# Seven block products instead of eight in a quarter of the down projection's K, in a one-core hybrid encoder layer

## The chip, the cores and the metric

The kernel runs on one core of one Trainium2 chip, in one launch. The metric is the device time of an execution in microseconds. The engines have short names in the profile: PE is TensorE (matmuls), PEld its weight loads, DVE is VectorE, ACT is ScalarE, POOL is GpSimd, SP is the engine that issues most DMAs.

## The reference, cut to what matters

One encoder layer over 256 tokens of width 2048, in float32. Three gated branches (a state-space mixer, dilated attention, a convolution module) are merged and projected; then comes the MLP, which is where the change is.

```python
h = rms_norm(x, norm1_g)
proj = h @ w_in                       # 2048 -> all branch inputs and gates
...                                   # three branches, gated and summed: merged
x = x + merged @ w_out
x = x + jnp.square(jax.nn.relu(rms_norm(x, norm2_g) @ w_mlp_up)) @ w_mlp_down
```

`w_mlp_up` is 2048 x 8192, `w_mlp_down` 8192 x 2048. Inputs and output are float32.

## The kernel before, in words

Weights are streamed from HBM in *units*: 256 rows of K by 512 columns, laid out as a tile of 128 partitions x 1024 (`raw`, 512 KB; two K chunks of 128 rows side by side). Each unit is split in two tiles of the matmul's own 32-bit type: ScalarE copies `raw` to `hi` (L1233) and VectorE subtracts, `lo = raw - hi` (`split_lo`, L254). Activations are kept as such pairs too. A product of two float32 values is then three matmuls: hi x hi, lo x hi and hi x lo (L1295, L1296, L1298 where the tokens are stationary and the weights stream, L1286, L1288, L1290 where the weights are stationary). A unit is 12 matmuls of 128x128 by 512 columns in the first mode (2 K chunks x 2 halves `t` of the tokens x 3); `ps` 0 runs the eight that need `hi`, then `ps` 1 the four that need `lo`.

Eight units make a *block*: a K of 2048 and 512 output columns for all 256 tokens, in two PSUM banks (`main`). The MLP's 8192 hidden values are cut in four parts r of 2048. An up block `("U", r, i)` gives 512 hidden values, and `job_up` turns them into squared ReLU activations `u` and their parts `ah`, `al` (one slab each, 4 K chunks x 256 tokens). A down block `("D", r, i)` multiplies part r's activations with 512 columns of the down weights, and `job_down` adds the result to `oacc[i]`, which began as x after the first half (`x` in the profile), and in the last part stores it. The order is U0 U1 D0 U2 D1 U3 D2 D3, each four blocks. A stretch of four down blocks is called a down stretch here.

The order of all instructions is written out by one loop over the units, with `k` the current unit (`for k in range(NU)`, L1326 on): load unit k+5 on SP's queue (`load`, L1215, 5 `raw` buffers), split unit k+3 (`LEAD` is 3; 4 `hi` and 4 `lo` buffers), run unit k's matmuls (`mm`), then let a planner (`Sched`) issue steps of the pending jobs behind them. So the `hi` of unit k+3 takes the buffer of unit k-1. Each engine runs its instructions in this order; semaphores hold what is not ready.

The planner's jobs are generators that yield their next need: `"v", n` or `"a", n` asks n ns of VectorE or ScalarE credit, `"w", n` waits n units, `"m", n` asks for n of 33 slabs of 4 KB a partition, `"b", n` for n of 4 PSUM banks, `"j", f` waits until f is true. A step of the highest priority (0: all MLP jobs) goes out while the credit is above 0, which it may then overdraw. Each unit ends with

```python
S.tick({"v": (2600 - 1140) * f * VSHARE, "a": (2600 - 950) * f * ASHARE, "g": 2600 * f, "p": 900})
...
self.credit[k] = min(self.credit[k] + g, CAP * max(g, 400.0))
```

with both shares 0.95 and `CAP` 1.2: a full unit brings VectorE a credit of 1387, and no more than 1664 are saved. `S.require` makes the planner issue whatever it takes, credit or not, until a condition holds (a slab, a bank or an accumulator that a job still has to give back).

PSUM has eight banks: two `main` tiles of two banks, used in turn (block b waits until block b-2 has been read), and four single banks (`pd`) for other work; the last block of all takes two of these.

Of the kernel before, what the change touches and what calls it, by code (L numbers as in the profile page):

```python
# [12 lines left out]
F32 = mybir.dt.float32  # L13
# [7 lines left out]
P = 128  # L21
# [169 lines left out]
def kernel(ctx: ExitStack, tc: tile.TileContext, xT, xn, par, cm, cd, cq, w1, wq, ws, out):  # L191
# [869 lines left out]
        st["rbc2"] = rb  # L1061


    act = {}

    def job_up(main, r, i):
        yield "m", 3
        u = slab([4, T], name="u")
        h = slab([4, T], F32R, name="ah")
        l = slab([4, T], F32R, name="al")  # L1070
        yield "j", lambda: "rbc2" in st
        yield "w", 1
        for e in range(2):
            yield "v", 680
            V.scalar_tensor_tensor(u[:, 2 * e:2 * e + 2, :], main[:, e, :].rearrange("p (a b) -> p a b", a=2), 0.0,
                                   st["rbc2"][:, None, :].to_broadcast([P, 2, T]), op0=ALU.max, op1=ALU.mult)
        st["main_free"].add(id(main))
        yield "w", 1
        yield "a", 1900
        A.activation(u, u, AF.Square)  # L1080
        A.activation(h, u, AF.Copy)
        yield "w", 1
        yield "v", 1150
        split_lo(l, u, h)
        S.give()
        act[r][0][i] = h
        act[r][1][i] = l

    def job_down(main, r, i):
        if r < 3:  # L1090
            yield "j", lambda: oacc[i] is not None
            yield "w", 1
            for t in range(2):
                yield "v", 620
                V.tensor_tensor(oacc[i][:, t, :], oacc[i][:, t, :], main[:, t, :], op=ALU.add)
            st["main_free"].add(id(main))
            return
        for t in range(2):
            V.tensor_tensor(oacc[i][:, t, :], oacc[i][:, t, :], main[:, t, :], op=ALU.add)  # L1099
            (nc.sync, nc.scalar)[t].dma_start(out[t * P:t * P + P, i * 512:i * 512 + 512], oacc[i][:, t, :])  # L1100
        st["main_free"].add(id(main))
        yield "w", 0


    st.update(h=([None] * 4, [None] * 4), ssd=([None] * 4, [None] * 4), conv=([None] * 4, [None] * 4),
              main_free=set(), conv_t=set(), q_blocks=0, att_n=0, ssd_c=[0] * 4, ssd_n=0, z_n=0, z_g=[False] * 4, mg_n=0,
              mgp=([None] * 4, [None] * 4), x2g=([None] * 4, [None] * 4))
    yss = cp.tile([P, 2, 4], F32, name="yss")
    st["yss"] = yss
# [67 lines left out]
    def up_block(r, i):  # L1177
        act.setdefault(r, ([None] * 4, [None] * 4))
        block("W", lambda: st["x2g"], lambda m: [(job_up(m, r, i), 0)],
              end=(lambda: S.give(8)) if (r == 3 and i == 3) else None)  # L1180

    def down_block(r, i):
        block("X", lambda: act[r], lambda m: [(job_down(m, r, i), 0)],
              end=(lambda: S.give(8)) if i == 3 else None)

    for o in ORDER:
        k, i = o[0], int(o[1])
# [7 lines left out]
        (up_block if k == "U" else down_block)(r, i)  # L1195


    units = [(bi, u) for bi, b in enumerate(blocks) for u in range(b["units"])]
    NU = len(units)
    raws, his, los = {}, {}, {}  # L1200

    def load(k):
        if k >= NU:
            return
        bi, u = units[k]
# [10 lines left out]
        raws[k] = t  # L1216

    def split(k):
        if k >= NU:
            return  # L1220
        bi, u = units[k]
        n = 2 * blocks[bi]["n"]
        h = hp.tile([P, 1024], F32R, tag="hi", name=nm("hi"))[:, :n]
        l = lp.tile([P, 1024], F32R, tag="lo", name=nm("lo"))[:, :n]
        r = raws.pop(k)
        if k == 0:
            for e in range(2):
                es = slice(e * n // 2, (e + 1) * n // 2)
                prep(e)
                A.activation(h[:, es], r[:, es], AF.Copy)  # L1230
                split_lo(l[:, es], r[:, es], h[:, es])
        else:
            A.activation(h, r, AF.Copy)  # L1233
            split_lo(l, r, h)
        his[k], los[k] = h, l
        S.on_split(k, n / 1024)

    mains = {}

    class Pair:  # L1240
# [5 lines left out]
        def __getitem__(self, at):  # L1246
            return self.of[at[1]][:, at[2]]

    def mm(k):
        bi, u = units[k]  # L1250
        b = blocks[bi]
        n, nk = b["n"], 2 * b["units"]
        if u == 0:
            if bi >= 2:
                j = mains[bi - 2]
                S.require(lambda: id(j) in st["main_free"], f"block {bi - 2} read")
                st["main_free"].discard(id(j))
            mains[bi] = pm.tile([P, 2, 512], F32, tag="main", name=nm("main")) if bi + 1 < len(blocks) \
                else Pair(bank(), bank())
        main = mains[bi]  # L1260
        wh = his.pop(k).rearrange("p (a b) -> p a b", a=2)
# [12 lines left out]
        first, last = kcs[0] == 0, kcs[1] == nk - 1  # L1274
        tail = bi == len(blocks) - 1 and u == b["units"] - 1
        order = [(ps, e, kc, t) for ps in range(2) for e, kc in enumerate(kcs) for t in range(2)]
        if tail:
            order.sort(key=lambda o: o[3])
        for ps, e, kc, t in order:
            ah, al = hi[kc // 4][:, kc % 4, :], lo[kc // 4][:, kc % 4, :]  # L1280
            if b["mode"] == "W":
                for c in (2 * t, 2 * t + 1):
                    o = main[:, t, (c % 2) * T:(c % 2) * T + T]
                    cs = slice(c * P, c * P + P)
                    if ps == 0:
                        PE.matmul(o, wh[:, e, cs], ah, start=(first and e == 0 and c % 2 == 0), stop=False,  # L1286
                                  skip_group_check=True)
                        PE.matmul(o, wh[:, e, cs], al, start=False, stop=False, skip_group_check=True)  # L1288
                    else:
                        PE.matmul(o, wl[:, e, cs], ah, start=False, stop=(last and e == 1), skip_group_check=True)  # L1290
            else:
                o = main[:, t, :n]
                xs_ = slice(t, T, 2) if b["perm"] else slice(t * P, t * P + P)
                if ps == 0:
                    PE.matmul(o, ah[:, xs_], wh[:, e, :], start=(first and e == 0), stop=False)  # L1295
                    PE.matmul(o, al[:, xs_], wh[:, e, :], start=False, stop=False)  # L1296
                else:
                    PE.matmul(o, ah[:, xs_], wl[:, e, :], start=False, stop=(last and e == 1))  # L1298
        if u == b["units"] - 1:
            if b["end"]:  # L1300
                b["end"]()
            for g, pr in b["post"](main):
                S.add(g, f"block{bi}", pr)

    S.take(8)
    st["xg"] = ([slab([4, T], F32R, name="xgh") for _ in range(4)], [slab([4, T], F32R, name="xgl") for _ in range(4)])
# [8 lines left out]

    for i in range(5):
        load_x(i)
        load(i)
    for i in range(LEAD):
        if i:  # L1320
            prep(2 * i)
# [2 lines left out]
    S.add(job_h(), "h", 0)  # L1324
    for k in range(NU):
        load_x(k + 5)  # L1326
        load(k + 5)
# [12 lines left out]
        bi, u = units[k]  # L1340
# [80 lines left out]
```

## Time and profile before

| | |
|---|---|
| three runs | 1958.81, 1959.17, 1960.99 us; median 1959.17 |
| the profiled execution | 1958.74 us, span of the trace 1957.0 us |
| granted TensorE clock | 0.999 |
| busy | PE 1945.3, PEld 1750.7, DVE 1302.9, ACT 1021.7, POOL 59.6 us |
| DMA | 373.03 MB, mean 191 GB/s |

Times in the profile count from the start of the span. A row of a group reads: line, engine, operation, output and inputs, shapes, count, then busy time in us and mean duration of one in ns, then the engine's idle time ahead of these instructions and what ended it. A row in time reads: start, duration, engine, line, operation; in brackets the idle time before it and what ended that. A row of a table by windows gives for each engine its busy time and its number of instructions in that stretch. Matmuls overlap in the array, so the duration of one is longer than the step from one start to the next.

### The profile page before, as it was taken

The page shows a single profiled execution, that of the slowest core. Times are in us where ns is not written, and L with a number is a line of the kernel's source. Part 1 is how long each engine was busy: PE and PEld are TensorE (multiplying, and loading weights), DVE is VectorE, ACT ScalarE, POOL GpSimd, SP SyncE. Part 2 cuts the span into 40 slices and gives each one's busy share as a digit, 9 for nine tenths or more (in the row PEclk, how much of TensorE's full clock was granted, in tenths as well). Part 3 has the DMA queues.
Part 4 walks back from the last instruction along what each step waited for, and adds up shares of the span by engine and source line. Part 5 has one row for each costly group of instructions (what it writes and reads, how often), then busy time and mean ns, then how long its engine had stood idle before and what let it go on. Part 6 is the DMA issues. An engine that isn't in the chain of part 4 may idle for free.

```text
span 1957.0 us, 29897 instructions
## 1 busy us (share of the span) xinstructions
PE 1945.3 (99%) x11738; PEld 1750.7 (89%) x11738; DVE 1302.9 (67%) x1878; ACT 1021.7 (52%) x1390; POOL 59.6 (3%) x74
## 2 busy tenths in 40 slices
PE   9999999999999999999999999999999999999999
PEld 9999999999989788888888888999988998998887
DVE  6688888787888888987655555555554554555444
ACT  7665586756666645544554444544443443444332
POOL 0000001000000000002000000000000000000000
PEclk9999999999999999999999999999999999999999
DMA  9575555565556555555565555555555555555554
GB/s 328 164 238 184 159 186 192 176 202 176 193 188 195 181 170 183 189 188 192 182 195 189 187 194 204 189 188 188 189 193 185 191 186 192 190 187 190 187 181 151
DMA packets 108174, 373.03 MB, mean 191 GB/s; under 512 B 12288, under 2 KB 13056, under 8 KB 108032
## 3 DMA queue, kind: packets, MB, share of 16 engines
q1 hardware_dynamic: 103904, 360.23, 55.8%
q0 software_dynamic: 2560, 8.39, 1.5%
q10 hardware_dynamic: 1568, 2.49, 0.4%
q8 instruction: 92, 1.51, 0.3%
q14 instruction: 50, 0.41, 0.1%
HBM read 368.84 MB, written 2.23 MB: 190 GB/s over the span
## 4 chain that ended last, share of the span: by engine, by line
PE 65%; DVE 0%; issue 0%
PE main L1295 15%; PE main L1296 15%; PE main L1298 15%; PE main L1286 6%; PE main L1290 6%; PE main L1288 6%; PE b L990 1%; PE b L1296 0%; PE b L1295 0%; PE b L1298 0%; DVE mg L973 0%; DVE x L1099 0%; PE b L608 0%; PE b L295 0%; PE b L635 0%
## 5 line engine op out<-in xcount | busy, mean ns | idle before, releaser
L254 DVE TENSOR_TENSOR lo<-raw,hi 128x1024 fp32r<-128x1024 f32 (+2 forms) x697 | 832.6, 1196 | 627.4 <-ACT hi L1233 622.1
L1233 ACT ACTIVATE hi<-raw 128x1024 fp32r<-128x1024 f32 (+2 forms) x695 | 715.2, 1031 | 855.6 <-PE main L1296 473.7
L1295 PE MATMUL main<-hi,hh 128*128 128x512 f32 (+1 forms) x800 | 303.4, 379 | 0.0
L1296 PE MATMUL main<-hi,hl 128*128 128x512 f32 (+1 forms) x800 | 297.3, 372 | 0.0
L1286 PE MATMUL main<-x2h,hi 128*128 128x256 f32 x1024 | 245.1, 280 | 0.0
L1288 PE MATMUL main<-x2l,hi 128*128 128x256 f32 x1024 | 244.3, 279 | 0.0
L1286 PE MATMUL main<-hh,hi 128*128 128x256 f32 x896 | 217.1, 282 | 2.8 <-ACT hi L1233 2.8
L1288 PE MATMUL main<-hl,hi 128*128 128x256 f32 x896 | 214.7, 280 | 0.0
L592 DVE SCALAR_TENSOR_TENSOR co<-cin,cpar,co 128x256 f32<-128x256 f32 x480 | 206.9, 483 | 0.0
L1298 PE MATMUL main<-lo,hh 128*128 128x512 f32 (+1 forms) x800 | 200.0, 372 | 0.0
L1288 PEld LDWEIGHTS main<-x2l,hi 128*128 128x128 f32 x1024 | 193.1, 189 | 0.2
L1286 PEld LDWEIGHTS main<-x2h,hi 128*128 128x128 f32 x1024 | 192.7, 188 | 0.2
L1295 PE MATMUL main<-hi,ah 128*128 128x512 f32 x480 | 188.9, 394 | 0.0
L1296 PE MATMUL main<-hi,al 128*128 128x512 f32 x480 | 188.6, 393 | 0.0
L1286 PEld LDWEIGHTS main<-hh,hi 128*128 128x128 f32 x896 | 169.1, 189 | 3.4 <-ACT hi L1233 3.2
L1295 PEld LDWEIGHTS main<-hi,hh 128*128 128x128 f32 x800 | 152.4, 190 | 21.7 <-issue 0.5
L1296 PEld LDWEIGHTS main<-hi,hl 128*128 128x128 f32 x800 | 152.5, 191 | 21.3 <-issue 0.9
L1288 PEld LDWEIGHTS main<-hl,hi 128*128 128x128 f32 x896 | 169.1, 189 | 0.2 <-issue 0.2
L1298 PEld LDWEIGHTS main<-lo,hh 128*128 128x128 f32 x800 | 147.8, 190 | 21.2
L1290 PE MATMUL main<-x2h,lo 128*128 128x256 f32 x1024 | 140.2, 280 | 0.0
L1298 PE MATMUL main<-lo,ah 128*128 128x512 f32 x480 | 130.1, 393 | 0.0
L1290 PEld LDWEIGHTS main<-x2h,lo 128*128 128x128 f32 x1024 | 128.5, 188 | 0.0
(242 smaller groups left out, 2255.9 us busy)
## 6 DMA issues: line engine op xcount, KB each, us to landing
raw<-ws_dram SPq DMA_DIRECT2D x600, 512.0 KB, 3.3
raw<-wq_dram SPq DMA_DIRECT2D x88, 384.0 KB, 3.2
fr<-sums POOLq DMA_DIRECT2D x32, 256.0 KB, 6.5
raw<-w_dram SPq DMA_DIRECT2D x7, 448.0 KB, 6.9
xr<-xn_dram SPq DMA_DIRECT2D x4, 512.0 KB, 7.9
x<-xn_dram SPq DMA_DIRECT2D x4, 512.0 KB, 4.3
xt<-xT_dram SPq DMA_DIRECT2D x7, 256.0 KB, 7.0
out_dram<-x SPq DMA_DIRECT2D x4, 256.0 KB, 3.6
```

Of the source, the lines that this page charges most:

```text
L254: V.tensor_tensor(lo, raw, hi.bitcast(F32), op=ALU.subtract)
L592: V.scalar_tensor_tensor(dst[:, e, :], x[:, e, k:k + T], par_("dw", (2 * i + e) * 31 + k), dst[:, e, :], op0=ALU.mult, op1=ALU.add)
L990: PE.transpose(b[:, e, t * P:t * P + P], src[:, t, k * P:k * P + P], ID)
L1233: A.activation(h, r, AF.Copy)
L1286: PE.matmul(o, wh[:, e, cs], ah, start=(first and e == 0 and c % 2 == 0), stop=False, skip_group_check=True)
L1288: PE.matmul(o, wh[:, e, cs], al, start=False, stop=False, skip_group_check=True)
L1290: PE.matmul(o, wl[:, e, cs], ah, start=False, stop=(last and e == 1), skip_group_check=True)
L1295: PE.matmul(o, ah[:, xs_], wh[:, e, :], start=(first and e == 0), stop=False)
L1296: PE.matmul(o, al[:, xs_], wh[:, e, :], start=False, stop=False)
L1298: PE.matmul(o, ah[:, xs_], wl[:, e, :], start=False, stop=(last and e == 1))
```

## The change

It rewrites only the down blocks, the accumulators and the planner's bookkeeping around them. The weights in HBM, their order in memory and every load's size stay.

Two neighbouring down blocks of a part (columns of i and i+1, i = 0 or 2) become one block of mode "Y", a *pair*. Of its eight K steps, steps 2 to 7 run as before, as *plain* units. In steps 0 and 1, that is, in a quarter of K, the four 512-column products of the two blocks are computed as a two-by-two block product (token halves x the two K chunks, times K chunks x the two column blocks) with seven block products in place of eight, in Winograd's form of Strassen's scheme. Each step becomes a *group* of four part-units that share the two raw tiles x (block i) and y (block i+1):

- part a: x is split as before; two products, one into the partial product p1, one straight into the first column block's accumulator. Behind the split, four sums of 128x512 are formed on VectorE: two in a slab `us`, one in place in y, one in place in x.
- part d: y, by now with its first half replaced by a sum, is split; two products.
- part b: `us` is split; two products.
- part c: the second half of x, by now a sum, is split (512 wide); one product.

So a group is 3 x (2 + 2 + 2 + 1) = 21 matmuls of 512 columns, where two units had 24. The stationary sides are the activations, or sums of their blocks, which `job_up` forms ahead for the first slab of each part (i = 0) in two slabs `sh`, `sl`, and which are kept until the part's last pair is done with them.

The units of a pair run in this order: four plain, a group, four plain, a group, four plain. The partial products p1, p5, p6, p7 take four more banks; with the two `main` tiles a pair thus has all eight. One pair has its accumulators in the `main` tiles and its partial products in the `pd` banks, the next the other way round; up blocks 2 and 3 of parts 1 to 3 take `pd` banks. `job_seven`, added after the second group's part c, reads the partial products: one copy on ScalarE and five additions or subtractions on VectorE, then three additions within SBUF, into `oacc`. `job_down` adds the accumulators as before; in the last part it waits until the pair's `job_seven` is done, and stores both token halves.

Loads follow the order of the raw tiles; x and y stay held until part c has been split. The planner's credit for VectorE is, per part-unit, `(2600 * e - 1140 * dv) * f * VSHARE` with (e, dv) = (0.5, 3.2) for a, (0.5, 1) for d and b, (0.25, 0.5) for c.

The core of the diff:

```diff
     def job_up(main, r, i):
...
+        if i == 0:
+            yield "m", 3
+            f = slab([4, 2, P], name="sf")
+            sh = slab([4, 2, P], F32R, name="sh")
+            sl = slab([4, 2, P], F32R, name="sl")
+            a = u.rearrange("p (q e) (t j) -> p t e q j", e=2, t=2)
+            for o, x, y_, op in ((0, a[:, 1, 0], a[:, 1, 1], ALU.subtract), (1, f[:, 0], a[:, 0, 0], ALU.subtract),
+                                 (2, a[:, 0, 0], a[:, 1, 0], ALU.subtract), (3, a[:, 0, 1], f[:, 1], ALU.add)):
+                yield "v", 400
+                V.tensor_tensor(f[:, o], x, y_, op=op)
+            yield "w", 1
+            yield "a", 950
+            A.activation(sh, f, AF.Copy)
+            yield "w", 1
+            yield "v", 1150
+            split_lo(sl, f, sh)
+            S.give()
+            acs[r] = sh, sl
...
+    def job_seven(p, done, i):
+
+        p1, p5, p6, p7 = p
+        yield "m", 1
+        tq = slab([2, 512], name="tq")
+        (c11, c21), (c12, c22) = [[oacc[i + e][:, t, :] for t in range(2)] for e in range(2)]
+        yield "w", 1
+        yield "a", 600
+        A.activation(tq[:, 0, :], p1, AF.Copy)
+        yield "v", 650
+        V.tensor_tensor(c11, c11, p1, op=ALU.add)
+        yield "v", 650
+        V.tensor_tensor(tq[:, 0, :], tq[:, 0, :], p6, op=ALU.add)
+        yield "v", 650
+        V.tensor_tensor(tq[:, 1, :], p5, tq[:, 0, :], op=ALU.subtract)
+        yield "v", 650
+        V.tensor_tensor(c21, c21, p7, op=ALU.add)
+        yield "v", 650
+        V.tensor_tensor(c22, c22, p7, op=ALU.subtract)
+        done()
+        for c, e in ((c21, 0), (c12, 1), (c22, 1)):
+            yield "v", 620
+            V.tensor_tensor(c, c, tq[:, e, :], op=ALU.add)
+        S.give()
+        st["seven"] += 1
...
+        for e, us in ((0, (2, 3)), (1, (2, 3)), (None, (0,)), (0, (4, 5)), (1, (4, 5)), (None, (1,)), (0, (6, 7)),
+                      (1, (6, 7))):
+            for u in us:
+                if e is None:
+                    order_ += [(bi, u), (bi, 8 + u)]
+                    for w in "adbc":
+                        units.append((bi, u, w, (len(order_) - 2, len(order_) - 1)))
+                else:
+                    order_.append((bi, 8 * e + u))
+                    units.append((bi, u + 8 * e, "n", (len(order_) - 1,)))
...
     def split(k):
...
+            if w in "na":
+                r = raws[rs[0]]
+            else:
+                r = {"d": raws[rs[1]], "b": sums[0], "c": raws[rs[0]][:, 512:]}[w]
             A.activation(h, r, AF.Copy)
             split_lo(l, r, h)
+        if w == "a":
+            S.require(lambda: S.mem >= 1, "slab for sums")
+            S.take()
+            sums[0] = slab([1024], name="us")
+            lo_, hi_ = slice(0, 512), slice(512, 1024)
+            x, y_, z = raws[rs[0]], raws[rs[1]], sums[0]
+            for o, p, q in ((z[:, lo_], x[:, lo_], y_[:, lo_]), (y_[:, lo_], y_[:, lo_], y_[:, hi_]),
+                            (z[:, hi_], z[:, lo_], y_[:, hi_]), (x[:, hi_], z[:, hi_], x[:, hi_])):
+                V.tensor_tensor(o, p, q, op=ALU.add)
...
+    def seven(k):
...
+        todo = {"a": ((A_(0, 0), f1, 0), (A_(1, 0), c1, 0)), "d": ((S_(3), f2, 1), (S_(4), c2, 0)),
+                "b": ((S_(1), f1, 1), (S_(2), f2, 0)), "c": ((A_(1, 1), c1, 1),)}[w]
+        for ps in range(2):
+            for i, ((xh, xl), o, t) in enumerate(todo):
+                cs = slice(512 * i, 512 * i + 512)
+                four = o is f1 or o is f2
+                if ps == 0:
+                    PE.matmul(o[:, t, :], xh, wh[:, cs], start=(four and u == 0), stop=False)
+                    PE.matmul(o[:, t, :], xl, wh[:, cs], start=False, stop=False)
+                else:
+                    PE.matmul(o[:, t, :], xh, wl[:, cs], start=False, stop=(four and u == 1))
...
-        S.tick({"v": (2600 - 1140) * f * VSHARE, "a": (2600 - 950) * f * ASHARE, "g": 2600 * f, "p": 900})
+        e, dv, da = {"n": (1, 1, 1), "a": (0.5, 3.2, 1), "b": (0.5, 1, 1), "d": (0.5, 1, 1), "c": (0.25, 0.5, 0.5)}[w]
+        S.tick({"v": (2600 * e - 1140 * dv) * f * VSHARE, "a": (2600 * e - 950 * da) * f * ASHARE, "g": 2600 * f * e,
+                "p": 900})
```

More of the change, by code (lines that the diff above doesn't have):

```diff
@@ L1061, in job_rms2, with free @@
         st["rbc2"] = rb
-    act = {}
+    act, acs = {}, {}
+    def free(main):
+        st["main_free"].add(id(main))
+        if isinstance(main, Pair):
+            S.banks += 2
     def job_up(main, r, i):
@@ L1076, in job_up @@
                                    st["rbc2"][:, None, :].to_broadcast([P, 2, T]), op0=ALU.max, op1=ALU.mult)
-        st["main_free"].add(id(main))
+        free(main)
         yield "w", 1
@@ L1097, in job_down @@
-            return
-        for t in range(2):
             V.tensor_tensor(oacc[i][:, t, :], oacc[i][:, t, :], main[:, t, :], op=ALU.add)
-            (nc.sync, nc.scalar)[t].dma_start(out[t * P:t * P + P, i * 512:i * 512 + 512], oacc[i][:, t, :])
-        st["main_free"].add(id(main))
-        yield "w", 0
+            if r == 3:
+                (nc.sync, nc.scalar)[t].dma_start(out[t * P:t * P + P, i * 512:i * 512 + 512], oacc[i][:, t, :])
+        free(main)
+    def job_seven(p, done, i):
[20 more added lines that the diff above has]
+            V.tensor_tensor(c, c, tq[:, e, :], op=ALU.add)
+        S.give()
+        st["seven"] += 1
@@ L1180, in up_block @@
               end=(lambda: S.give(8)) if (r == 3 and i == 3) else None)
+        blocks[-1]["apart"] = r > 0 and i >= 2
     def down_block(r, i):
-        block("X", lambda: act[r], lambda m: [(job_down(m, r, i), 0)],
-              end=(lambda: S.give(8)) if i == 3 else None)
+        if i % 2 == 0:
+            block("Y", lambda: act[r], None, units=16)
+            blocks[-1].update(r=r, i=i)
     for o in ORDER:
@@ L1247, in __getitem__, with pm_tile, pd_pair @@
             return self.of[at[1]][:, at[2]]
+    pms = []
+    def pm_tile():
+        if len(pms) >= 2:
+            j = pms[-2]
+            S.require(lambda: id(j) in st["main_free"], "accumulators read")
+            st["main_free"].discard(id(j))
+        pms.append(pm.tile([P, 2, 512], F32, tag="main", name=nm("main")))
+        return pms[-1]
+    def pd_pair():
+        S.require(lambda: S.banks >= 2, "banks read")
+        S.banks -= 2
+        return Pair(bank(), bank())
     def mm(k):
-        bi, u = units[k]
+        bi, u, w, _ = units[k]
         b = blocks[bi]
         n, nk = b["n"], 2 * b["units"]
[L1253 to L1259, printed above, removed]
+        pair = b["mode"] == "Y"
+        if bi not in mains:
+            if pair:
+                S.require(lambda: b["r"] in acs, "sums of activations")
+                make = pm_tile if b["i"] == 0 else pd_pair
+                mains[bi] = [make(), make()]
+            else:
+                mains[bi] = (pd_pair if b.get("apart") else pm_tile)()
+        if w != "n":
+            if (u, w) == (0, "a"):
+                make = pd_pair if b["i"] == 0 else pm_tile
+                b["four"] = [make(), make()]
+            seven(k)
+            return
         main = mains[bi]
+        if pair:
+            j, u = divmod(u, 8)
+            main = main[j]
+            nk = 16
         wh = his.pop(k).rearrange("p (a b) -> p a b", a=2)
@@ L1273, in mm @@
         hi, lo = parts(b["key"])
-        first, last = kcs[0] == 0, kcs[1] == nk - 1
-        tail = bi == len(blocks) - 1 and u == b["units"] - 1
+        first, last = kcs[0] == (4 if pair else 0), kcs[1] == nk - 1
+        tail = k == NU - 1
         order = [(ps, e, kc, t) for ps in range(2) for e, kc in enumerate(kcs) for t in range(2)]
@@ L1298, in mm @@
                     PE.matmul(o, ah[:, xs_], wl[:, e, :], start=False, stop=(last and e == 1))
-        if u == b["units"] - 1:
+        if pair:
+            if u == 7:
+                if j == 1 and b["i"] == 2:
+                    S.give(8)
+                S.add(job_down(main, b["r"], b["i"] + j), "down", 0)
+        elif u == b["units"] - 1:
             if b["end"]:
@@ L1317 @@
         load_x(i)
-        load(i)
+        load_upto(i)
     for i in range(LEAD):
@@ L1326 @@
         load_x(k + 5)
-        load(k + 5)
+        load_upto(k + 5)
         if k + LEAD < 8:
```

74 lines of the change are left out of this document (57 added, 17 removed).

## The prediction, made before the changed kernel was run

> **What bounds the kernel now.** I read the page's first two parts, then the chain of work that ended last, then a table by windows of the four down-projection stretches, then single instructions in time.
>
> ```profile
> PE 1945.3 (99%) x11738; PEld 1750.7 (89%) x11738; DVE 1302.9 (67%) x1878; ACT 1021.7 (52%) x1390; POOL 59.6 (3%) x74
> ...
> PE 65%; DVE 0%; issue 0%
> ```
>
> TensorE is busy in 1945.3 of 1957.0 us, and the chain is TensorE work with nothing to speak of from the others. But a busy share is an average, so the stretches that change are read alone.
>
> ```profile
> core 0: us, PE busy (x) PEld busy (x) DVE busy (x) ACT busy (x) POOL busy (x), PEclk, DMA share, GB/s
> 1419.10:1507.30 88.20, 88.20 (x383) 71.57 (x382) 45.13 (x41) 35.16 (x34) 0.00 (x0) 1.00 0.57 191
> 1600.50:1688.20 87.70, 87.70 (x390) 71.83 (x389) 44.31 (x40) 35.05 (x34) 0.00 (x0) 1.00 0.57 192
> 1777.50:1865.60 88.10, 88.10 (x383) 71.55 (x382) 44.36 (x41) 35.83 (x34) 0.00 (x0) 1.00 0.58 189
> 1865.60:1952.90 87.30, 87.23 (x381) 71.09 (x379) 40.42 (x39) 29.36 (x28) 0.00 (x0) 1.00 0.48 165
> ```
>
> In all four, TensorE has no idle time that counts and the full granted clock (1.00), weight loading leaves room, VectorE is half used (45.13 of 88.20 us), ScalarE 40%, the DMA engines 57%. So a matmul taken out there comes off the end, as long as the other engines stay ahead. What one matmul costs is not its duration (they overlap) but the step from one start to the next:
>
> ```profile
> 1419.13 0.40 PE L1295 MATMUL main<-hi,ah 128*128 128x512 f32 x1
> ...
> 1508.15 0.28 PE L1286 MATMUL main<-x2h,hi 128*128 128x256 f32 x1
> ```
>
> These are the first matmul of the first down stretch and the first of the up block behind it: 89.02 us for 4 blocks x 8 units x 12 = 384 matmuls, 231.8 ns each. Now one unit in detail:
>
> ```profile
> 1842.39 0.40 PE L1295 MATMUL main<-hi,ah 128*128 128x512 f32 x1
> ...
> 1844.01 0.39 PE L1296 MATMUL main<-hi,al 128*128 128x512 f32 x1
> ...
> 1844.23 1.08 PE L1298 MATMUL main<-lo,ah 128*128 128x512 f32 x4
> 1844.43 1.06 ACT L1233 ACTIVATE hi<-raw 128x1024 fp32r<-128x1024 f32 x1 [1.70 <-PE main L1296]
> ...
> 1845.15 0.39 PE L1295 MATMUL main<-hi,ah 128*128 128x512 f32 x1
> ...
> 1845.53 1.23 DVE L254 TENSOR_TENSOR lo<-raw,hi 128x1024 fp32r<-128x1024 f32 x1 [0.34 <-ACT hi L1233]
> ```
>
> A unit steps in 2.76 us (1842.39 to 1845.15), 230.0 ns a matmul; I use 231 ns, between the two. Three things more are to be seen. The last of the four L1298 starts at about 1844.92 and the next unit's first follows one step later: a unit boundary costs nothing. The ScalarE copy starts when the eighth matmul of the unit ends (1844.01 + 0.39 = 1844.40), as its hi buffer is then free, 0.92 us before the unit's steps end. And the lo, behind it on VectorE, ends 1.84 us after the unit's steps end (1845.53 + 1.23 - 1844.92), for a unit that TensorE reaches three units later. That lead of 6 us or more is the cover of all that follows.
>
> **The change, part by part.** *Matmuls removed.* In each of 4 down stretches, 2 chunk pairs, 2 K steps (units 0 and 1): two units of 12 become 3 x (2 + 2 + 2 + 1) = 21. So 16 groups x 3 = 48 matmuls less, all 128x512: 48 x 0.231 = 11.1 us, on the path. That is the gain and its upper bound; nothing else leaves TensorE.
>
> *Units cut smaller.* 64 part-units (a, d, b, c) in place of 32 whole ones: 32 boundaries more. By the row above they cost nothing. The dearest nearest row is a separate wait instruction in TensorE's queue:
>
> ```profile
> L1295 PEldq EVENT_SEMAPHORE  x3: 51/51/51, 684.7 to 694.8; - x3
> ```
>
> 32 x 51 ns = 1.6 us is the upper end; I take 0, as boundaries in these stretches show no such wait.
>
> *Work added to VectorE and ScalarE.* Prices, from the groups of VectorE and of ScalarE in the last two down stretches, and one group of the whole span for an addition of two 512-wide operands in SBUF:
>
> ```profile
> L254 DVE TENSOR_TENSOR lo<-raw,hi 128x1024 fp32r<-128x1024 f32 x61 | 74.5, 1225 | 79.3 <-ACT hi L1233 77.2 <-PE b L1296 2.1
> L1095 DVE TENSOR_TENSOR x<-x,main 128x512 f32<-128x512 f32 x8 | 5.1, 680 | 0.0
> L1099 DVE TENSOR_TENSOR x<-x,main 128x512 f32<-128x512 f32 x6 | 3.9, 683 | 3.9 <-PE main L1298 3.9
> L1075 DVE SCALAR_TENSOR_TENSOR u<-main,rbc 128x512 f32<-128x512 f32 x2 | 1.3, 680 | 0.0
> ```
>
> ```profile
> L1233 ACT ACTIVATE hi<-raw 128x1024 fp32r<-128x1024 f32 x60 | 63.3, 1059 | 100.7 <-PE main L1296 81.5 <-DMA raw<-ws_dram 9.0 <-DVE x L1099 8.7
> L1081 ACT ACTIVATE ah<-u 128x1024 fp32r<-128x1024 f32 x1 | 1.1, 1059 | 0.0
> L1080 ACT ACTIVATE u<-u 128x1024 f32<-128x1024 f32 x1 | 1.0, 1042 | 0.0
> ```
>
> ```profile
> L879 DVE TENSOR_TENSOR em<-em 128x512 f32<-128x512 f32 x16 | 11.0, 691 | 1.3 <-ACT em L872 0.3
> ```
>
> VectorE, per group: 3.5 lo in place of 2 (3 x 1.23 + 0.69 - 2 x 1.23 = 1.92) and 4 weight sums of 128x512 (4 x 0.69 = 2.76), so 4.7 us, x16 = 75. Per pair 8 additions at 0.68 = 5.4, x8 = 44. Per stretch, in the up stage before it, 4 sums of activations (256 wide, at most the 0.69 of 512) and a lo of 1.22, 4.0, x4 = 16. Together 135 us, all beside TensorE's work, if no single one is late. A pair takes 12 x 2.77 + 42 x 0.231 = 42.9 us, and two of them a stretch; VectorE's share there goes from 45 in 88 to about 45 + 19 + 11 = 75 in 86 us. ScalarE gets 1.5 hi per group and per pair a copy of half a hi's width, about 0.6, some 35 us in all with the four copies of the activation sums; never near its limit.
>
> *Is any of it late?* Zero is TensorE's start on part a; four plain units of 2.77 lie before it (ends at -8.31, -5.54, -2.77, 0), and a, d, b end at 1.39, 2.77, 4.16, c at 4.85. There are four hi and four lo buffers, so each part takes that of the unit four before it, at the times the unit above shows. hi(a) -9.23 to -8.17; lo(a) to -6.90; the sums to -4.14. hi(d) needs the second sum (-5.52), ends -4.46; lo(d) -2.91. hi(b) takes the third plain unit's buffer, -3.69 to -2.63; lo(b) -1.35. hi(c) -0.92 to -0.3; lo(c) 0.69. The next plain unit takes a's buffer: hi 0.92 (two thirds of a) to 1.98, lo to 3.25. Wanted: d at 1.39, b at 2.77, c at 4.16, the plain unit at 4.85. The smallest lead is 2.9 us, at the plain unit behind the group. In the first group after an up stage the last block's activations are in the way: two L1075 (0.68 each) ahead of lo(a); then, as the sums need a slab that only those activations give back, a square and a copy on ScalarE (1.04 and 1.06) and one lo ahead of the sums. The sums then end at -1.73, hi(d) at -2.05, lo(c) at 1.42, and the plain unit's hi still at 1.98: still 2.9 us. I cost it at nothing; without this cover each group would pay what it is late.
>
> *Accumulators.* Each pair takes eight banks, and the next block's first four are those that the pair's partial products held, read by six instructions that begin after the second c. The planner gives each VectorE job credit: a plain unit brings 1387 (at most 1664 saved), part a takes 2231, d and b bring 152, c 76. So 1664 before the group falls to -567, -415, -263, -187; the first plain unit brings 1200, and two additions of 650 go out; the second brings 1287, two more; the third 1374, the last one, and the banks count as free, before the fourth unit is issued. In time, from the end of c: the lo of the fourth plain unit ends 2.2, two additions 3.6, a lo 4.8, two additions 6.2, a lo 7.4, the last 8.1. The next block starts at 4 x 2.77 = 11.08: 3.0 us ahead of need. Nothing.
>
> *Loads.* Same bytes and the same 512 KB pieces, but both raw buffers of a group stay held until lo(c) has read the second column half (0.69). Behind that the SP queue loads the plain unit 4 after the group and the next group's first piece.
>
> ```profile
> raw<-ws_dram SPq DMA_DIRECT2D x600, 512.0 KB, 3.3
> ...
> out_dram<-x SPq DMA_DIRECT2D x4, 256.0 KB, 3.6
> ```
>
> 0.7 + 3.3 = 4.0, with two in flight perhaps 6; the fourth plain unit's hi can't start before part c's buffer is free, at 4.6, and TensorE reaches that unit at 4.85 + 3 x 2.77 = 13.2. Nothing. In the last stretch the first pair's output DMAs wait on SP and ScalarE behind both blocks' additions; the raws of the next group are queued ahead of them, and hi of the unit four ahead is put back to about 6.3 us after the end of the pair's last unit but one, 4.7 us before TensorE wants it. Nothing.
>
> *The end.*
>
> ```profile
> 1951.51 0.69 DVE L1099 TENSOR_TENSOR x<-x,b 128x512 f32<-128x512 f32 x1 [8.26 <-PE b L1298]
> ...
> 1952.22 0.34 SPq L1100 DMA_DIRECT2D out_dram<-x  x1
> 1952.87 0.69 DVE L1099 TENSOR_TENSOR x<-x,b 128x512 f32<-128x512 f32 x1 [0.67 <-PE b L1298]
> 1953.59 0.34 ACTq L1100 DMA_DIRECT2D out_dram<-x  x1
> ```
>
> The last halves are added and stored as before. But block 2's two stores now go out some 3 us before block 3's last instead of 20 us, since its last unit is two units before the end and three of the pair's additions precede it. With 3.6 us a landing they overlap the last store a little: 0 to 1.5 us, and I take 0.4, near the lower end, as only the last part of one store overlaps.
>
> *Sum.* The profiled execution took 1958.74 us (span 1957.0 and 1.74 around it): 1958.74 - 11.1 + 0.4 = 1948.0. The median of the runs shown, 1959.17, lies 0.43 higher: 1948.5.
>
> The Trainium skill's page "TensorE: Matmul & The Clock Gate", section "Back-to-back issue gap", speaks against this size: it gives about 131 ns a matmul for a sustained stream of weight loads and matmuls of 512 columns. By it 48 of them are worth 6.3 us and the time would be 1953.3. The trace disagrees with it, 231 ns in all 384 steps counted; I go by the trace.
>
> **The rivals.**
> *Part of the gain is lost in the groups* (small waits at part boundaries, about 0.1 us at each of 64, or VectorE late by 0.4 us in each of 16 groups): 6.4 us back, 1954.9 - against it, boundaries that cost nothing and 2.9 us of lead; for it, VectorE's share of nearly nine tenths around the groups and the longer chain copy, lo, sums, copy. With half as much, 1951.7.
> *The gain is cancelled or more by the accumulators: slower.* If the reads of the partial products go out only when the next block asks for their banks, they stand behind the lo that ends 1.84 us into that block, and five additions of 0.68 follow: TensorE waits 5.2 us at each of 7 pair ends (the eighth has no block behind it), 36.7 us, 1985. It decides from 11.1 / 7 = 1.6 us a pair on, which is 4.6 us later than my reckoning. The credit that falls to -567 speaks for it, the 1387 a plain unit against it. By the same page of the Trainium skill, section "Part 1: The HAM clock gate", idleness beyond some 3.4 us halves TensorE's clock, which would add to this; no row here shows such a gap.
> *A removed matmul brings less than the mean step.* If the step were held by something other than the streaming of its columns, what goes could be as little as its weight load, 71.57 us / 382 = 187 ns in the first window: 9.0 us, 1950.6, still inside the forecast's own range. What speaks against it is that weight loading has room in all four windows. The figure of the page named above would leave 1953.3, and no row supports it.
> *No change within the measurement*: a mix of late groups that returns 8 to 14 us, about 1959.
>
> **How the numbers follow.** A kernel measured here can be told from no change at about 0.2%, 3.9 us, so 1955.2 divides faster from same. The forecast (1947.0 to 1950.5) has 0.78; the partial loss 0.11, nearly all still faster; a step worth less than 187 ns 0.01; no change 0.05; slower 0.05. Faster 0.88, same 0.07, slower 0.05. The low end is the full 11.1 with no tail and the spread of the runs, the high end takes in the boundaries (1.6), the tail (1.5) and half the partial loss: 1946.8 to 1953.5.
>
> **What the profile of the changed kernel would show.** TensorE's matmuls 48 fewer, about 11690; each down stretch from its first matmul to the next stage 89.0 - 12 x 0.231 = 86.2 us; a group from a to the plain unit behind it 4.85 us against 5.54; TensorE's busy time equal to its window in all four; VectorE near 1438 us in all; the six reads of the partial products ending about 8 us after c. I am wrong if TensorE shows idle time before part d or before the plain unit behind a group (the sums are late), before the first matmul of a block (accumulators), or before hi at a raw (loads); or if the step of the part-units is not 231 ns.

## The result, and the profile after

| | before | changed |
|---|---|---|
| median | 1959.16 us (4 runs, 1958.81 to 1960.99) | 1949.19 us (4 runs, 1948.74 to 1949.48) |
| ratio, 95% interval | | 0.9947, 0.9930 to 0.9964 |
| profiled execution, span | 1958.74, 1957.0 us | 1948.74, 1947.0 us |

The change makes the kernel 10.0 us faster; 1948.5 was forecast. First the page of the changed kernel, parts 1 and 4:

```profile
PE 1935.5 (99%) x11690; PEld 1741.8 (89%) x11690; DVE 1419.1 (73%) x2058; ACT 1054.8 (54%) x1434; POOL 59.6 (3%) x74
...
PE 65%; DVE 0%; issue 0%
```

There are 48 matmuls fewer (11738 before), VectorE is 116 us busier, and the chain that ended last names TensorE for 65% of the span and nothing else to speak of, as before. The four down stretches in a table by windows (busy us and instructions of each engine, TensorE clock, DMA share, GB/s):

```profile
core 0: us, PE busy (x) PEld busy (x) DVE busy (x) ACT busy (x) POOL busy (x), PEclk, DMA share, GB/s
1419.10:1505.20 86.10, 86.10 (x374) 69.89 (x373) 70.73 (x80) 43.09 (x45) 0.00 (x0) 1.00 0.60 195
1594.90:1680.60 85.70, 85.70 (x373) 69.82 (x372) 70.66 (x80) 43.01 (x45) 0.00 (x0) 1.00 0.59 196
1770.20:1856.30 86.10, 86.10 (x374) 69.73 (x373) 70.51 (x80) 43.06 (x45) 0.00 (x0) 1.00 0.58 195
1856.30:1942.80 86.50, 86.50 (x374) 69.95 (x372) 68.53 (x80) 37.31 (x39) 0.00 (x0) 1.00 0.53 171
```

TensorE is busy for the whole of each window while VectorE's share went from a half to 82%: the added work is covered. How far the first stretch shrank is read from its first matmul and the first of the up block behind it, and the last two stretches from their first matmul (in the kernel before, then in the changed one) to the last addition:

```profile
1419.10 0.39 PE L1425 MATMUL main<-hi,ah 128*128 128x512 f32 x1
...
1505.30 0.28 PE L1416 MATMUL main<-x2h,hi 128*128 128x256 f32 x1
```

```profile
1775.74 0.39 PE L1295 MATMUL main<-hi,ah 128*128 128x512 f32 x1
```

```profile
1770.18 0.40 PE L1425 MATMUL main<-hi,ah 128*128 128x512 f32 x1
...
1942.89 0.69 DVE L1121 TENSOR_TENSOR x<-x,b 128x512 f32<-128x512 f32 x1 [0.70 <-PE b L1428]
```

The first stretch takes 86.20 us instead of 89.02 (2.82 less; 86.2 was forecast), the second, read in the same way, 85.86 instead of 88.57 (2.71). The last two together take 172.71 from the first matmul to the last addition (1942.89 - 1770.18) where they took 177.13 (1952.87 - 1775.74): 4.42 less, for 24 matmuls that at 231 ns are 5.5. The sum is 9.95 of the 10.0 us. The up stretches between did not move (89.5 us each), nor did the end: 4.1 us from the last addition to the end of the span in both.

Now one group in time, the second of the first pair. Part a starts at 1446.21, the plain unit behind the group at 1451.09:

```profile
1437.17 1.06 ACT L1322 ACTIVATE hi<-raw 128x1024 fp32r<-128x1024 f32 x1 [0.99 <-PE main L1426]
...
1440.13 0.69 DVE L1332 TENSOR_TENSOR raw<-raw 128x512 f32<-128x512 f32 x1
...
1440.99 1.06 ACT L1322 ACTIVATE hi<-raw 128x1024 fp32r<-128x1024 f32 x1 [2.76 <-PE main L1428]
...
1441.45 0.69 DVE L1332 TENSOR_TENSOR raw<-us,raw 128x512 f32<-128x512 f32 x1
...
1446.21 0.39 PE L1457 MATMUL b<-hi,ah 128*128 128x512 f32 x1
...
1446.48 0.69 DVE L254 TENSOR_TENSOR lo<-raw,hi 128x512 fp32r<-128x512 f32 x1 [1.39 <-PE main L1428]
1447.38 1.06 ACT L1322 ACTIVATE hi<-raw 128x1024 fp32r<-128x1024 f32 x1 [1.21 <-PE main L1458]
...
1451.09 0.39 PE L1425 MATMUL main<-hi,ah 128*128 128x512 f32 x1
...
1458.16 0.68 DVE L1144 TENSOR_TENSOR x<-x,b 128x512 f32<-128x512 f32 x1
```

Counted from 1446.21: hi(a) starts at -9.04 (reckoned -9.23); then come the ends: the last sum at -4.07 (-4.14), hi(d) at -4.16 (-4.46), lo(c) at 0.96 (0.69), the plain unit's hi at 2.23 (1.98). TensorE takes the plain unit up at 4.88 (4.85). The last read of the partial products ends 7.75 us after part c (8.1). The bracket of hi(d) names TensorE, though what it waited for is the second sum, which ends at 1440.82 (1440.13 + 0.69): of several waits the profile names one.

### The profile page after: what moved, and what is told of

Its sections match the earlier page's. It is cut to its first block, busy times and chain, and to the rows that moved or that the text cites. A ratio compares the mean times of both kernels' runs of the same rounds, so it can differ in the third digit from the quotient of the medians.

```text
span 1947.0 us, 30117 instructions
## 1 busy us (share of the span) xinstructions
PE 1935.5 (99%) x11690; PEld 1741.8 (89%) x11690; DVE 1419.1 (73%) x2058; ACT 1054.8 (54%) x1434; POOL 59.6 (3%) x74
## 3 DMA queue, kind: packets, MB, share of 16 engines
HBM read 368.84 MB, written 2.23 MB: 191 GB/s over the span
## 4 chain that ended last, share of the span: by engine, by line
PE 65%; DVE 0%; issue 0%
PE main L1425 12%; PE main L1426 12%; PE main L1428 12%; PE main L1416 4%; PE main L1420 4%; PE main L1418 4%; PE b L1416 2%; PE b L1420 2%; PE b L1418 2%; PE b L1426 2%; PE b L1428 2%; PE b L1425 2%; PE b L1457 1%; PE main L1457 1%; PE main L1460 1%; PE b L1460 1%
## 5 line engine op out<-in xcount | busy, mean ns | idle before, releaser
L254 DVE TENSOR_TENSOR lo<-raw,hi 128x1024 fp32r<-128x1024 f32 (+3 forms) x713 | 842.7, 1185 | 504.5 <-ACT hi L1322 479.8
L1322 ACT ACTIVATE hi<-raw 128x1024 fp32r<-128x1024 f32 (+3 forms) x711 | 723.8, 1022 | 804.3 <-PE main L1426 323.9
L1416 PE MATMUL main<-x2h,hi 128*128 128x256 f32 x640 | 153.3, 280 | 0.0
L1418 PE MATMUL main<-x2l,hi 128*128 128x256 f32 x640 | 152.7, 279 | 0.0
L1420 PE MATMUL main<-hh,lo 128*128 128x256 f32 x896 | 123.6, 280 | 0.2 <-DVE lo L254 0.2
L1418 PEld LDWEIGHTS main<-x2l,hi 128*128 128x128 f32 x640 | 120.7, 189 | 0.2
L1416 PEld LDWEIGHTS main<-x2h,hi 128*128 128x128 f32 x640 | 120.4, 188 | 0.2
L1420 PEld LDWEIGHTS main<-hh,lo 128*128 128x128 f32 x896 | 113.1, 189 | 0.4 <-DVE lo L254 0.4
L1416 PE MATMUL b<-x2h,hi 128*128 128x256 f32 x384 | 91.8, 280 | 0.0
L1418 PE MATMUL b<-x2l,hi 128*128 128x256 f32 x384 | 91.6, 279 | 0.0
```

The lines of the kernel that those rows point to most:

```text
L254: V.tensor_tensor(lo, raw, hi.bitcast(F32), op=ALU.subtract)
```

## The experiments

Theory A: the gain is the number of matmuls taken out times their step; all added work lies beside TensorE; and the missing 1.1 us in the last two stretches is a longer step of the remaining matmuls that comes from where their operands lie in memory, since the new slabs `sh`, `sl`, `us`, `tq` push all later ones to other places. Theory B: VectorE's work lengthens the step or makes small waits.

| kernel | median us | ratio to before, 95% interval |
|---|---|---|
| no_sums | 1949.31 | 0.9954, 0.9939 to 0.9969 |
| c_twice | 1960.14 | 1.0005, 0.9995 to 1.0014 |
| c_none | 1937.59 | 0.9892, 0.9877 to 0.9906 |
| shift1 | 1947.83 | 0.9945, 0.9930 to 0.9959 |
| sums_plus2 | 1948.07 | 0.9946, 0.9931 to 0.9961 |
| sums_plus6 | 1961.94 | 1.0016, 1.0007 to 1.0025 |
| seven_late | 1984.28 | 1.0129, 1.0112 to 1.0146 |
| adjacent | 1951.73 | 0.9963, 0.9948 to 0.9978 |
| aligned | 1951.78 | 0.9964, 0.9951 to 0.9977 |
| offset192 | 1936.84 | 0.9888, 0.9871 to 0.9904 |
| before_aligned | 1962.65 | 1.0021, 1.0012 to 1.0031 |
| weights64 | 1935.58 | 0.9887, 0.9871 to 0.9904 |

**no_sums.** The four sums of a group are made on one column instead of 512, and part b splits x as loaded.

```diff
-                r = {"d": raws[rs[1]], "b": sums[0], "c": raws[rs[0]][:, 512:]}[w]
+                r = {"d": raws[rs[1]], "b": raws[rs[0]], "c": raws[rs[0]][:, 512:]}[w]
...
-                V.tensor_tensor(o, p, q, op=ALU.add)
+                V.tensor_tensor(o[:, 0:1], p[:, 0:1], q[:, 0:1], op=ALU.add)
```

> The four weight sums of each group are made on one column instead of 512 (and part b multiplies x as loaded), so VectorE has 16 x 4 x some 0.6 = 38 us less to do; matmuls, their order and all slabs stay. Theory A (the sums are hidden; a matmul's step depends on where its operands lie): within 0.5 us of the changed kernel, 1949.2, mean step in the last two down stretches 231.7 ns as there. Theory B (VectorE's extra work lengthens the step or makes small waits): the step goes back to the 230.2 ns of the kernel before, about 1948.1 us.

VectorE is 33 us less busy (1385.9), and nothing else moves:

```profile
1420.00 0.39 PE L1425 MATMUL main<-hi,ah 128*128 128x512 f32 x1
...
1506.20 0.28 PE L1416 MATMUL main<-x2h,hi 128*128 128x256 f32 x1
```

86.20 us again for the first stretch, 1949.31 in all. Taken one by one in the two traces, the 1488 steps of the four stretches differ by 0.00 ns on average with a spread of 0.11 ns, while along the trace they vary by 3.3 ns. So taking 33 us off VectorE moves no step at all, and each matmul has a step of its own that comes back in another execution of another kernel with the same memory layout. Theory B falls for the sums; the rest of VectorE's added work (splits and additions) stays in this run, and is settled by the pair of aligned kernels below.

**c_twice, c_none.**

```diff
-                "b": ((S_(1), f1, 1), (S_(2), f2, 0)), "c": ((A_(1, 1), c1, 1),)}[w]
+                "b": ((S_(1), f1, 1), (S_(2), f2, 0)), "c": ((A_(1, 1), c1, 1),) * 2}[w]
...
-                cs = slice(512 * i, 512 * i + 512)
+                cs = slice(0, 512) if w == "c" else slice(512 * i, 512 * i + 512)
```

So c_twice computes part c's product twice. In c_none the tuple of part c is empty, and its product is left out.

> Part c's product is computed twice (added twice into the accumulator): 24 matmuls a group as before the change, with all of the change's work on VectorE and ScalarE. Theory A: 48 matmuls x 0.231 = 11.1 us more than the changed kernel, 1960.3, i.e. the time before plus about 1 us, and no wait on TensorE. A rival in which part of the gain came from the new order or from the accumulators: clearly less than 11.1 us more, at or under 1957.

> Part c's product is left out, its split stays: 18 matmuls a group. Theory A: 11.1 us less than the changed kernel, 1938.1; the lead at the plain unit behind a group shrinks from 2.9 to 2.2 us and still covers. A rival in which the splits are nearly late: the group takes what VectorE takes, and less than 11 us is saved.

10.95 us more and 11.6 us less than the changed kernel: 228 and 242 ns for each of 48 matmuls, both ways about the step that was forecast. In the traces, which have less spread than the medians, the four stretches grow by 11.1 us and shrink by 11.5. With eight products the whole change is worth nothing (1.0005, 0.9995 to 1.0014): within some 2 us, the new order, the accumulators and VectorE's work neither bring nor cost anything. These are prices of a whole matmul with its weight load, as the prediction took them. The Trainium skill's page "TensorE: Matmul & The Clock Gate", section "Back-to-back issue gap", gives about 131 ns for such a stream; these two runs disagree with it, at 228 and 242.

**shift1.** One more slab is held from the first to the fourth up block.

```diff
+        if (r, i) == (0, 0):
+            S.take(1)
+            held[0] = [slab([4, T], name="dm") for _ in range(1)]
+            for d in held[0]:
+                V.memset(d[:, 0, 0:1], 0.0)
...
+        if (r, i) == (0, 3):
+            for d in held[0]:
+                V.memset(d[:, 0, 0:1], 0.0)
+            S.give(1)
```

> One more slab is held during the first up stage (a write of one column at its start and end), nothing else: every later slab, so the stationary activations of all four down stretches, lies at another address. Theory A: the mean step in the last two stretches changes by 0.5 ns or more in some direction, with each slab keeping one step in all blocks that use it, and the time moves by 0.5 to 4 us. Theory B: the step stays at 231.7 ns and the time at 1949.2.

The steps, one by one, no longer have anything to do with those of the changed kernel (correlation 0.05, where no_sums has 1.00), so they do hang on the layout. The size was a miss: the means move by only 0.2 ns in the last two stretches (231.9 to 231.7) and 0.5 ns in the first two (231.3 to 230.8), and 1947.83 against 1949.19 is within what runs of one kernel spread over. Moving slabs by one place deals the steps anew; it does not make them shorter on the whole.

**sums_plus2, sums_plus6, adjacent** probe the lead.

```diff
-                            (z[:, hi_], z[:, lo_], y_[:, hi_]), (x[:, hi_], z[:, hi_], x[:, hi_])):
+                            *[(z[:, hi_], z[:, lo_], y_[:, hi_])] * 7, (x[:, hi_], z[:, hi_], x[:, hi_])):
```

```diff
-        for e, us in ((0, (2, 3)), (1, (2, 3)), (None, (0,)), (0, (4, 5)), (1, (4, 5)), (None, (1,)), (0, (6, 7)),
+        for e, us in ((0, (2, 3)), (1, (2, 3)), (None, (0,)), (None, (1,)), (0, (4, 5)), (1, (4, 5)), (0, (6, 7)),
```

The first is sums_plus6 (sums_plus2 has 3 for 7), the second adjacent.

> The third weight sum of each group is made three times: VectorE has 2 x 0.69 = 1.4 us more ahead of part d's lo. My lead table: lo(d) ends at -1.5 where TensorE wants it at 2.3, lo(c) and the plain unit's parts do not move; no wait, 1949.2 within 0.5 us. The rival (VectorE is all but late at nine tenths of the time): 1.4 us a group, up to 22 us.

> The third weight sum is made seven times: 4.1 us more a group. By the lead table alone still 1.1 us early (lo(d) at 1.2 against 2.3). But VectorE then has 45.5 us of work in a pair that TensorE does in 42.9, so the lead is used up from pair to pair: between 3 and 20 us more than the changed kernel, 1952 to 1969, TensorE waiting for lo or hi inside the groups. If the groups had no lead to spend, 16 x 4.1 = 66 us more.

> The two groups of a pair follow each other with no plain units between (order: four plain, group, group, eight plain). By the lead table the second group's lo(d) ends 7.25 us after the first a starts where TensorE wants it at 7.2, and lo(b), lo(c) are about on time: 0.1 to 0.3 us a pair, 1950 to 1952. The rival, in which the plain units between are what pays for the groups: VectorE's 14.3 us of work against TensorE's 9.7 in the two groups, 2 to 4.6 us a pair, 1965 to 1986.

Two more sums a group cost nothing and leave TensorE without any wait in the stretches. Six more cost 12.8 us, in the middle of the range, and the longest waits of TensorE in the stretches name lo, as they should (in total us, times, longest):

```profile
PE main L1460 <- DVE lo L254: 3.8, 4, 2.3
PE b L1460 <- DVE lo L254: 3.1, 4, 1.1
```

These eight waits are 6.9 of the 12.8 us. The rest lies in steps of 0.26 to 0.52 us beside and between them, and behind the longest wait, 2.3 us, in steps of 0.43 us: there the granted clock was 0.51 for 3.4 us.

In adjacent TensorE stands still 0.2 to 0.3 us in each of the eight pairs, 2.2 us in all, at the place the table gave, the lo of part d in the second group (here the second pair's):

```profile
1479.86 1.23 DVE L254 TENSOR_TENSOR lo<-raw,hi 128x1024 fp32r<-128x1024 f32 x1
...
1481.14 0.19 PEld L1460 LDWEIGHTS main<-lo,sh 128*128 128x128 f32 x1 [0.44 <-DVE lo L254]
```

So the plain units between the groups are worth some 2 us, and not the 16 us or more of the rival; the four buffers ahead do most of the covering.

**seven_late.**

```diff
-        yield "w", 1
+        yield "w", 9
         yield "a", 600
         A.activation(tq[:, 0, :], p1, AF.Copy)
```

> job_seven waits nine units instead of one before its first step, so the planner issues the reads of the partial products only when the next block asks for their banks. This makes the slower rival of the prediction: five additions of 0.68 behind the lo that ends 1.84 us into the block: TensorE waits 5.2 us at each of 7 pair ends, 36.7 us more, 1986. If the accumulators do not hold TensorE up: 1949.2.

1984.28: 35.1 us more than the changed kernel where 36.7 was reckoned. But the sum is right for a wrong reason. TensorE's longest waits in this kernel:

```profile
PE b L1425 <- DVE x L1136: 8.3, 4, 2.1
PE main L1416 <- DVE tq L1140: 7.0, 2, 3.5
PE b L1425 <- ACT hi L1322: 3.7, 1, 3.7
PE main L1425 <- DVE tq L1140: 3.5, 1, 3.5
```

Seven waits at pair ends, as reckoned, but of 2.1 us (where the next block's first bank held p1 alone, whose last reader is L1136) or 3.5 us (where its first tile held p1 and p5, read last by L1140), 18.8 us in all, not 7 x 5.2: the first matmul asks for its own bank or tile only. A further 3.7 us is a hi in the last stretch that came late because the output stores stood ahead of raw loads on SP: the stores went out from 1939.15, the loads behind them from 1940.80, and the hi waited 4.8 us for its raw. The rest is for the most part the clock. The stretch behind the first of the 2.1 us waits, and behind the third:

```profile
1464.00:1470.00 6.00, 5.89 (x25) 4.62 (x26) 5.05 (x9) 1.06 (x1) 0.00 (x0) 1.00 0.26 92
...
1832.00:1838.00 6.00, 6.00 (x20) 4.71 (x20) 3.62 (x6) 1.06 (x1) 0.00 (x0) 0.72 0.25 87
```

Behind the third TensorE is busy all the time but is granted 0.72 of its clock, and single steps are 0.43 us. The profiled execution is 36.2 us longer than the changed kernel's; 22.5 us are the waits, and the steps behind these eight waits add up to some 14 us too long. The clock was lower behind three of the four waits of 2.1 us, all three of 3.5 us and the one of 3.7 us. The kernel before shows it too: behind a wait of 2.27 us that ends at 684.8, the granted clock is 0.50 from 685.1 to 688.5. The Trainium skill's page "TensorE: Matmul & The Clock Gate", section "Part 1: The HAM clock gate", has this halving after idleness of some 3.4 us. Here waits of 2.1 to 2.3 us were enough, though not each time.

**aligned, offset192, before_aligned, weights64.** Can the long steps be avoided? Slabs were 4160 bytes apart, so, counted modulo 256, they began at 0, 64, 128 and 192, while the raw, hi and lo tiles all began at 0. Some steps in the traces were 226.7 ns long, and the theory put these down to slabs at multiples of 256; that it was these slabs is not shown here. The runs make all slabs 4096 bytes long. One tile had needed the 64 extra bytes, the padded input of the 5-tap convolution (the diff is that of aligned):

```diff
+    pad = cp.tile([P, 16], F32, name="pad")
...
-        xp = slab([4, 260], name="xp")
+        xp = slab([4, T], name="xp")
...
-                V.scalar_tensor_tensor(xq[:, k, :], xp[:, k, j:j + T], par_("cw5", c * 5 + j),
-                                       xq[:, k, :], op0=ALU.mult, op1=ALU.add)
+                a, b = max(0, 2 - j), T - max(0, j - 2)
+                V.scalar_tensor_tensor(xq[:, k, a:b], xp[:, k, a + j - 2:b + j - 2], par_("cw5", c * 5 + j),
+                                       xq[:, k, a:b], op0=ALU.mult, op1=ALU.add)
```

In aligned and before_aligned `pad`, 64 bytes, stands ahead of the slabs, in offset192 behind them; weights64 has one in each place.

> The changed kernel with slabs of 4096 bytes instead of 4160 (the one tile that needed more, the padded input of the 5-tap convolution, is kept without its pads and the taps run over shorter ranges) and 64 bytes ahead of them, so that every slab begins at a multiple of 256 bytes in its partition. The theory that a matmul's step hangs on where its stationary operand lies: in the traces so far, matmuls with both token parts at multiples of 256 step in 226.7 ns once settled, others in 228 to 236. So all 512-column matmuls go to about 226.7, in the down stretches 1488 x 4.8 ns = 7 us, over some 4270 of them about 17 us: 1932; with the 256-column ones moving too, down to 1915. If the alignment is nothing: 1949 as before.

> The same with the 64 bytes behind the slabs instead of ahead: every slab is 4096 bytes and begins 192 bytes past a multiple of 256; raw, hi and lo tiles lie as in the kernel with aligned slabs. Theory: the steps stay near 230 ns as between slabs of that class in the traces so far, 1949 within 3 us. If it is the slabs' size or the changed convolution that helps and not the alignment: the time of the aligned kernel.

> The kernel before the change with the same aligned slabs. Theory: about 1942 (down to 1925), and against the aligned changed kernel 48 x 0.2267 = 10.9 us more: the change is worth the same number of matmuls at a shorter step.

The first matmuls of the first down stretch, of the up stretch behind it and of the next down stretch, for aligned and for offset192:

```profile
1423.39 0.40 PE L1425 MATMUL main<-hi,ah 128*128 128x512 f32 x1
...
1507.74 0.28 PE L1416 MATMUL main<-x2h,hi 128*128 128x256 f32 x1
...
1599.89 0.40 PE L1425 MATMUL main<-hi,ah 128*128 128x512 f32 x1
```

```profile
1414.70 0.40 PE L1426 MATMUL main<-hi,ah 128*128 128x512 f32 x1
...
1501.50 0.28 PE L1417 MATMUL main<-x2h,hi 128*128 128x256 f32 x1
...
1588.56 0.39 PE L1426 MATMUL main<-hi,ah 128*128 128x512 f32 x1
```

Aligned slabs do what was expected where activations are stationary, 84.35 us / 372 = 226.7 ns for 512 columns, against 231.7 in the first stretch of the changed kernel. But where they stream past stationary weights, 92.15 / 768 = 120.0 ns for 256 columns against 116.6, and there are 5760 such matmuls: 1951.78, slower, not 1932. My theory looked at the stationary operand alone and falls. With slabs 64 bytes short of a multiple of 256, which was to change nothing, 256 columns take 87.06 / 768 = 113.4 ns and 512 columns 233.3 ns in the first stretch and 228.9 in the others: 1936.84, 12 us better than the changed kernel. The kernel before with aligned slabs misses its forecast of 1942 for the same reason (1962.65), but stands 10.9 us above aligned, as expected. Its first down stretch:

```profile
1425.68 0.40 PE L1295 MATMUL main<-hi,ah 128*128 128x512 f32 x1
...
1512.75 0.28 PE L1286 MATMUL main<-x2h,hi 128*128 128x256 f32 x1
```

That is 87.07 us / 384 = 226.7 ns, the same step as in aligned; over all four stretches the means of the two are equal to 0.01 ns, and the last two differ by 5.44 us, 24 whole steps. So where the slabs of both kernels all lie alike, at multiples of 256, nothing is missing from the last two stretches, although aligned has all of VectorE's added work. That leaves the layout as the cause of the missing 1.1 us, and the change is worth its 48 matmuls on either layout.

The last run moves the weight tiles as well: the slabs are at multiples of 256 as in aligned, but their distance from the weight tiles is as in offset192.

> The kernel with aligned slabs, with 64 more bytes between the slabs and the raw, hi and lo tiles: slabs at multiples of 256, the weight tiles 64 past them, so the distance between the two kinds is again 64 short of a multiple of 256 as in the kernel with slabs at 192. If the step hangs on the distance alone: 229.3 ns for 512 columns and 115.4 for 256, about 1937. If on the activations' place alone: 226.7 and 120.0, 1952. If on the stationary operand's place where that is an activation and on the distance where it is a weight: 226.7 and 115.4, about 1926.

```profile
1413.47 0.40 PE L1428 MATMUL main<-hi,ah 128*128 128x512 f32 x1
...
1500.27 0.28 PE L1419 MATMUL main<-x2h,hi 128*128 128x256 f32 x1
...
1587.34 0.39 PE L1428 MATMUL main<-hi,ah 128*128 128x512 f32 x1
```

86.80 and 87.07 us: to 0.01 us the steps of offset192, not those of aligned. Moving one kind of operand by 64 bytes changes the steps, moving both does not: in these runs, what counts is how the stationary and the streamed operand lie to each other, not where either lies. The distance modulo 256 is not the whole of it, as under the same distance 512 columns take 233.3 ns in the first stretch and 228.9 in the others; what lies behind it stays open. At 1935.58 us weights64 is as fast as offset192 within the spread of the runs, 0.9887 of the kernel before. That ratio is the change and the layout together: the kernel before was not run in this layout.

## Why the prediction was right

- *Matmuls removed times their step*: the mechanism is shown by c_twice and c_none, and the size of 11.1 us holds for the matmuls themselves (48 x 230.8 = 11.1 with the mean step of all 1536 before). The mis-sized term is the step of those that stay: I carried 231 ns over to the changed kernel. It went from 230.8 to 231.6 ns (344.6 us over the four stretches / 1488), 1.2 us back, nearly all in the last two stretches, where it went from 230.4 to 231.9. no_sums excludes the weight sums as the cause, shift1 shows that the layout deals the steps anew, and the two aligned kernels, whose steps are alike, show that it is the layout and not VectorE.
- *Boundaries at nothing*: right; steps at the boundaries of part-units are 232.1 ns on average where the others are 231.5, and the upper end of 1.6 us was not needed.
- *VectorE, ScalarE and loads at nothing*: right, and the table of leads was right to 0.3 us. Most of that difference is one misread: the row has the copy start 0.72 us before the unit's steps end (1844.43 against 1845.15), not 0.92, and the lo end 1.61 us after that, not 1.84, which was counted from the start of the last matmul. The smallest lead, at the plain unit's hi, was thus 2.65 us and not 2.9. sums_plus2 spends 1.4 us of part d's lead for nothing, sums_plus6 more than there is over a pair. VectorE's total came out at 1419 us instead of 1438. The 16 sums of activations took 6.8 us where I had put the upper bound of 11. Most of the rest is counting: the durations of VectorE's instructions add up to 130 us more than before, near my 135, but successive ones overlap in the records (the second sum above ends at 1440.82, the third starts at 1440.74), and busy time counts such a stretch once.
- *Accumulators at nothing*: right (7.75 us after c, of 11.1). The rival's price had the right sum, 35.1 for 36.7, by luck: waits of 2.1 to 3.5 us instead of 5.2 make 18.8, and a late hi (3.7) and the lower clock behind the waits, which I left out of the sum, happen to make up the rest.
- *The end*: 0.4 us was put in and 0 came.

## What to carry to other kernels

When one engine is busy throughout and the work taken from it is counted in its own steps, the forecast is the count times the step, and the effort belongs in a table of when each buffer comes free and each part is ready: here it told to a few tenths of a microsecond which orders would wait. Measure the step from start to start over a stretch, not the duration of one matmul, and expect it to move when tiles change places: by 0.3% with this change, by 2 to 3% when all slabs moved. Before cutting the algorithm further, try where the two operands lie: 64 bytes between slabs and weight tiles brought 16 us (1951.78 to 1935.58), more than this change.

## What the runs showed of the hardware that I had not expected

- The step of a matmul depends on how its stationary and its streamed operand lie to each other within the partition: with slabs and weight tiles all at multiples of 256 bytes 226.7 ns for 512 columns and 120.0 for 256; at 64 bytes short of that 229 to 233 and 113 to 118; with slabs at all multiples of 64, 224 to 241 for single steps of 512 columns and 231 and 116.6 on average. It came back step by step in another execution with the same layout (no_sums). Why, and what other distances would give, stays open; the best of both, 226.7 and 113.4, was not reached in one kernel.
- A pause of 2.1 us was enough, three times in four, for TensorE's clock to be halved over some ten matmuls of 512 columns (0.72 granted over 6 us).
